# Layer norm: accumulated sums and ScalarE squares in place of VectorE's statistics

## Chip, cores and metric

The kernel runs on one core of a Trainium2 chip. The metric is the device time of one execution in microseconds, as the median of several runs. A profile of one execution goes with it; its span runs from the first recorded event to the last.

## What is computed

A two-layer decoder trunk on 512 tokens of width 1024, all in float32. Layer 1 is gated linear attention with memory cross-attention, layer 2 stick-breaking attention with memory cross-attention. After each mixer and after each PEER expert stage stands a layer norm over the scaled residual, four in all:

```python
def layer_norm(x, g, b):
    xf = x.astype(jnp.float32)
    mu = jnp.mean(xf, axis=-1, keepdims=True)
    var = jnp.mean(jnp.square(xf - mu), axis=-1, keepdims=True)
    return ((xf - mu) * lax.rsqrt(var + EPS) * g + b).astype(x.dtype)

for layer in range(DEPTH):
    mix = gla_layer_mixer(...) if layer < N_A_LAYERS else sb_layer_mixer(...)
    h = layer_norm(DEEPNORM_ALPHA * h + mix, ln_g[layer, 0], ln_b[layer, 0])
    ffn = peer(h, peer_w_q[layer], peer_subkeys[layer], peer_u[layer], peer_v[layer])
    h = layer_norm(DEEPNORM_ALPHA * h + ffn, ln_g[layer, 1], ln_b[layer, 1])
```

## The kernel before

The residual stream lies in SBUF as `E.x` (tile name `xnat`): 128 partitions, four token tiles of 128 tokens, 1024 columns each. For matmuls it is kept transposed as well, split into a high and a low float32r part (`xhi`, `xlo`), so that each product is three matmuls: high by high, low by high, high by low. `x_to_T` makes those parts of one token tile: eight transposes on TensorE (L813), the high part on ScalarE (L817), the low part on VectorE (L818).

`layer_norm(E, lp, t, halves, gam, bet)` works on one token tile, 128 rows of 1024. `halves` are the two 512-column halves of what is added to the residual, in PSUM (`oacc`, `acc`) or, for one tile, in SBUF (`va`). For each half VectorE forms `y = ALPHA*x + half` (L830) and takes its statistics (L831). One aggregate (L832) gives mean and variance, L834 adds epsilon, ScalarE takes the square root (L835), and VectorE meanwhile writes the centred and scaled `y` over itself (L836). The reciprocal (L837) is refined by one Newton step (L839 to L842), and L843 writes the result to `E.x`. The table for the root is asked for early by `warm_sqrt` (L847); where another table has been loaded in between, a load stands before the root.

It is called 16 times:

- `out_proj_ln`, after each mixer: the output projection runs tile by tile on TensorE (L248 to L252, into `oacc`), in an order written out by hand: tile t's matmuls, then the transposes of tile t-1, while tile t's norm runs on the other engines. After tile 3 TensorE first does the early part of the next stage's query projection (`pq`, L113 to L115, three tiles of tokens), and then tile 3's transposes. VectorE and ScalarE are ordered by the framework's scheduler there. The load of the next stage's keys (L998) stands on ScalarE's queue.
- `peer`, at the end of each stage, through `finish`. Token tile 0 is done by gathered expert rows, which VectorE accumulates into `va` (L985) after its dot products (L967); the other three tiles by dense matmuls over all 16384 experts (into `acc`). The last five expert blocks of every tile are held back, so that the tiles end one after the other: TensorE does tile 1's five blocks, its norm follows, then tile 2's, then tile 3's, with transposes of the finished tiles between. Tile 0's norm stands in the hand-written order of VectorE and ScalarE; those of the other tiles are ordered by the scheduler, which may weave them into it. In the second stage nothing is transposed, and each finished tile goes to the output by a transfer on SyncE's queue (L1320).

After the first PEER stage mixer B starts with weights that ScalarE and VectorE split as well (L93, L94) and whose first matmuls are `bsp`, L113 to L115.

Of the kernel before, what the change touches and what calls it, by code (L numbers as in the profile page):

```python
# [9 lines left out]
F32 = mybir.dt.float32  # L10
# [3 lines left out]
AF = mybir.ActivationFunctionType  # L14
ALU = mybir.AluOpType
AX = mybir.AxisListType
P = 128
T = 512
NT = 4
D = 1024  # L20
NC = 8
ALPHA = 4.0 ** 0.25
EPS = 1e-5
# [195 lines left out]
def out_proj_ln(E, cat, wo, lng, lnb, ahead, order=range(NC), rows=None):  # L219


    nc = E.nc
    with E.tc.tile_pool(name="lp", bufs=1, reuse_waits="tile") as lp:
        w = {}
        for c in order:
            w[c] = split(E, load_raw(E, wo[c], "wo"), "wo", lp, f"wo{c}", rows=None if rows is None or c >= GH else rows[:, c:c + 1])
        gam, bet = load_ln(E, lp, lng, lnb)
        warm_sqrt(E)
        next(ahead)
        with E.tc.manual_schedule(engines={mybir.EngineType.PE}):  # L230
            for t in range(NT + 1):
                if t < NT:
                    acc = [psum(E, name="oacc") for h in range(2)]
                    for c in order:
                        ch, cl = cat[c]
                        mov_mm(E, acc, ch[:, t * P:(t + 1) * P], cl[:, t * P:(t + 1) * P], *w[c], c == order[0], c == order[-1])
                if t == NT:
                    next(ahead)
                if t > 0:
                    x_to_T(E, t - 1)  # L240
                if t < NT:
                    layer_norm(E, lp, t, acc, gam, bet)
# [578 lines left out]
def layer_norm(E, lp, t, halves, gam, bet):  # L821

    nc = E.nc
    y = lp.tile([P, D], F32, tag="lny", name="lny", bufs=2)
    st = E.lnp.tile([P, 2, 6], F32, tag="lnst", name="lnst", bufs=2)
    mv = E.lnp.tile([P, 2], F32, tag="lnmv", name="lnmv", bufs=2)
    sm = E.lnp.tile([P, 4], F32, tag="lnsm", name="lnsm", bufs=2)
    for hf in range(2):
        sl = slice(hf * 512, (hf + 1) * 512)
        nc.vector.scalar_tensor_tensor(y[:, sl], E.x[:, t, sl], ALPHA, halves[hf], op0=ALU.mult, op1=ALU.add)  # L830
        nc.vector.bn_stats(st[:, hf], y[:, sl])  # L831
    nc.vector.bn_aggr(mv, st)  # L832
    ve, sd, r0, q = (sm[:, i:i + 1] for i in range(4))
    nc.vector.tensor_scalar(ve, mv[:, 1:2], EPS, None, op0=ALU.add)  # L834
    nc.scalar.activation(sd, ve, AF.Sqrt)  # L835
    nc.vector.scalar_tensor_tensor(y, y, mv[:, 0:1], gam, op0=ALU.subtract, op1=ALU.mult)  # L836
    nc.vector.reciprocal(r0, sd)  # L837

    nc.vector.tensor_mul(q, r0, r0)  # L839
    nc.vector.tensor_mul(q, q, ve)  # L840
    nc.vector.tensor_scalar(q, q, -0.5, 1.5, op0=ALU.mult, op1=ALU.add)
    nc.vector.tensor_mul(r0, r0, q)  # L842
    nc.vector.scalar_tensor_tensor(E.x[:, t], y, r0, bet, op0=ALU.mult, op1=ALU.add)  # L843
# [44 lines left out]
def peer(E, mixer, wq, sk, ut, vt, un, lng, lnb, out_dram=None):  # L888
# [6 lines left out]
    with ExitStack() as pp:  # L895
# [421 lines left out]
        def finish(t, halves):  # L1317
            layer_norm(E, wv, t, halves, *vp["ln"])
            if out_dram is not None:
                nc.sync.dma_start(out_dram[t * P:(t + 1) * P], E.x[:, t])  # L1320
# [154 lines left out]
```

## Time and profile before

| | |
|---|---|
| median of 3 runs | 3024.09 us (3017.12 to 3024.11) |
| the profiled execution | 3013.86 us |
| its span | 3012.1 us |
| TensorE matmul busy | 2930.4 us, 97% |
| VectorE busy | 2397.6 us, 80% |
| ScalarE busy | 1429.3 us, 47% |
| GpSimd busy | 646.5 us, 21% |

In the lines of the profile PE is TensorE's matmul, PEld its weight load, DVE VectorE, ACT ScalarE, POOL GpSimd, SP SyncE; a "q" behind the name is that engine's queue of waits and transfers. A timeline row gives the start in us, the duration in us, the engine, the line of the kernel, the operation, and "out<-in" by tile names with shapes; a bracket tells how long the engine had been idle before and which instruction released it. A row of a tile's list gives the count and the shortest, median and longest duration in ns. A busy TensorE is not TensorE at its peak; idle time of an engine that is not the bottleneck costs nothing. Instructions of one engine overlap slightly, so the distance from start to start is less than the duration.

### The profile page before, as it was taken

Reading aid. Unit: us, or ns where it says so; the run is one execution under the profiler, and the core shown is the slowest. Engines: PE = TensorE matmul, PEld = TensorE weight load, DVE = VectorE, ACT = ScalarE, POOL = GpSimd, SP = SyncE. Lnnn points to the kernel's source line nnn. Section 1 sums busy time; section 2 is a strip of 40 time slices with the busy share of each in tenths; the row PEclk is TensorE's granted clock in tenths of the full one; section 3 lists DMA queues with packets and bytes.
Section 4 is the critical chain, followed back from the end, with each engine's and each line's share of the span. In section 5 each row is a group of like instructions: output and inputs, shape, how many; then the busy total and the mean of one; then the engine's idle time right before and its main releaser. Section 6 shows DMA issues by size and latency. Waiting matters only on the chain.

```text
span 3012.1 us, 44494 instructions
## 1 busy us (share of the span) xinstructions
PE 2930.4 (97%) x16250; PEld 2589.2 (86%) x16250; DVE 2397.6 (80%) x5289; ACT 1429.3 (47%) x2482; POOL 646.5 (21%) x560
## 2 busy tenths in 40 slices
PE   9999999999999999999899899999999999999997
PEld 7878899999998888888676588999999998888886
DVE  5565899999876888787756658999999778787888
ACT  5342457676773333433235423466676643333332
POOL 0100131222323222322002000321213233223221
PEclk9999999999999999999899999999999999999999
DMA  4331488888999999999310223789889899999995
GB/s 175 112 105 63 155 294 316 320 313 318 334 336 323 308 346 357 347 352 346 126 63 29 76 79 119 276 309 323 304 324 321 330 330 333 338 341 347 369 341 190
DMA packets 314555, 789.91 MB, mean 262 GB/s; under 512 B 41808, under 2 KB 133984, under 8 KB 307936
## 3 DMA queue, kind: packets, MB, share of 16 engines
q1 hardware_dynamic: 216384, 419.48, 40.4%
q0 software_dynamic: 73728, 268.47, 25.2%
q10 hardware_dynamic: 24224, 99.13, 8.4%
q8 instruction: 127, 2.08, 0.3%
q14 instruction: 92, 0.75, 0.1%
HBM read 692.09 MB, written 94.90 MB: 261 GB/s over the span
## 4 chain that ended last, share of the span: by engine, by line
PE 91%; DVE 6%; issue 1%; DMA 1%; ACT 1%; ACTq 0%; SPq 0%; DVEq 0%
PE ph L113 11%; PE acc L248 11%; PE acc L250 11%; PE acc L252 11%; PE ph L115 11%; PE ph L114 11%; PE pq L114 2%; PE pq L115 2%; PE pq L113 2%; PE pg L1204 1%; PE pg L1205 1%; PE pss L1252 1%; PE bsp L113 1%; PE bsp L114 1%; PE bsp L115 1%
## 5 line engine op out<-in xcount | busy, mean ns | idle before, releaser
L113 PE MATMUL ph<-xhi,uh 128*128 128x384 f32 x2048 | 701.0, 342 | 0.0
L115 PE MATMUL ph<-xhi,ul 128*128 128x384 f32 x2048 | 686.3, 335 | 0.2
L114 PE MATMUL ph<-xlo,uh 128*128 128x384 f32 x2048 | 685.5, 335 | 0.0
L93 ACT ACTIVATE vh<-vr 128x1024 fp32r<-128x1024 f32 x256 | 271.5, 1060 | 597.0 <-issue 422.2
L932 POOL DMA_INDIRECT gr<-in_un,gidx x256 | 300.5, 1174 | 1023.2 <-DVE gr L967 806.8
L248 PE MATMUL acc<-vh,whi 128*128 128x512 f32 x1536 | 475.4, 391 | 8.9 <-ACT whi L1354 8.9
L250 PE MATMUL acc<-vl,whi 128*128 128x512 f32 x1536 | 474.4, 390 | 0.0
L252 PE MATMUL acc<-vh,wlo 128*128 128x512 f32 x1536 | 473.9, 390 | 0.0
L932 POOL DMA_INDIRECT gr<-in_vt,gidx x256 | 294.5, 1150 | 808.3 <-DVE va L985 736.8
L94 DVE TENSOR_TENSOR vl<-vr,vh 128x1024 fp32r<-128x1024 f32 x256 | 313.6, 1225 | 184.7 <-ACT vh L93 184.7
L93 ACT ACTIVATE uh<-ur 128x1024 fp32r<-128x1024 f32 x288 | 304.6, 1057 | 243.6 <-PE ph L114 234.1
L94 DVE TENSOR_TENSOR ul<-ur,uh 128x1024 fp32r<-128x1024 f32 x288 | 350.6, 1218 | 65.1 <-ACT uh L93 65.0
L114 PEld LDWEIGHTS ph<-xlo,uh 128*128 128x128 f32 x2048 | 386.0, 188 | 0.0
L113 PEld LDWEIGHTS ph<-xhi,uh 128*128 128x128 f32 x2048 | 385.7, 188 | 0.0
L115 PEld LDWEIGHTS ph<-xhi,ul 128*128 128x128 f32 x2048 | 385.0, 188 | 0.9 <-DVE ul L94 0.9
L248 PEld LDWEIGHTS acc<-vh,whi 128*128 128x128 f32 x1536 | 288.8, 188 | 70.6 <-ACT whi L1354 11.2
L250 PEld LDWEIGHTS acc<-vl,whi 128*128 128x128 f32 x1536 | 288.7, 188 | 61.2 <-DVE vl L94 1.3
L252 PEld LDWEIGHTS acc<-vh,wlo 128*128 128x128 f32 x1536 | 288.6, 188 | 60.5 <-DVE wlo L1355 0.9
L985 DVE SCALAR_TENSOR_TENSOR va<-gr,gw,va 128x1024 f32<-128x1024 f32 x254 | 325.3, 1281 | 15.7 <-DMA gr<-in_vt,gidx 15.4
L967 DVE SCALAR_TENSOR_TENSOR gr<-gr,xnat 128x1024 f32<-128x1024 f32 x256 | 310.4, 1214 | 11.7 <-DMA gr<-in_un,gidx 11.6
L1177 ACT ACTIVATE obl<-obh,rat 128x128 f16<-128x128 f16 x768 | 244.3, 393 | 20.0 <-ACT gt L1208 6.5
L1354 ACT ACTIVATE whi<-w 128x384 fp32r<-128x384 f32 x256 | 130.6, 510 | 59.5 <-DVE w L1351 59.5
(333 smaller groups left out, 4154.5 us busy)
## 6 DMA issues: line engine op xcount, KB each, us to landing
ur<-in_ut SPq DMA_DIRECT2D x256, 512.0 KB
vr<-in_vt SPq DMA_DIRECT2D x256, 512.0 KB
Gd<-gt ACTq DMA_DIRECT2D x48, 1024.0 KB
gl<-Gd SPq DMA_DIRECT2D x30, 1536.0 KB
Ad<-act ACTq DMA_DIRECT2D x108, 384.0 KB
al<-Ad SPq DMA_DIRECT2D x108, 384.0 KB
ur<-in_wq SPq DMA_DIRECT2D x32, 512.0 KB
bs<-in_b_st SPq DMA_DIRECT2D x14, 512.0 KB
```

Source lines behind the costliest of these rows:

```text
L93: nc.scalar.activation(hi, raw, AF.Copy)
L94: sub = lambda: eng.tensor_sub(lo, raw, hi.bitcast(F32))
L113: nc.tensor.matmul(ps, h, xhi[:, c, sl], start=(c == 0), stop=False)
L114: nc.tensor.matmul(ps, h, xlo[:, c, sl], start=False, stop=False)
L115: nc.tensor.matmul(ps, l, xhi[:, c, sl], start=False, stop=(c == NC - 1))
L248: nc.tensor.matmul(acc[hf], lh, hi[:, hf * 512:(hf + 1) * 512], start=first, stop=False)
L250: nc.tensor.matmul(acc[hf], lh, lo[:, hf * 512:(hf + 1) * 512], start=False, stop=False)
L252: nc.tensor.matmul(acc[hf], ll, hi[:, hf * 512:(hf + 1) * 512], start=False, stop=last)
L932: nc.gpsimd.indirect_dma_start(out=gr, out_offset=None, in_=tab, in_offset=bass.IndirectOffsetOnAxis(ap=gidx[:, k:k + 1], axis=0))
L967: nc.vector.scalar_tensor_tensor(gr, gr, 1.0, E.x[:, 0], op0=ALU.mult, op1=ALU.mult, accum_out=gh[:, k:k + 1])
L985: nc.vector.scalar_tensor_tensor(va, gr, gw[:, k:k + 1], va, op0=ALU.mult, op1=ALU.add)
L1177: nc.scalar.activation(obl[:, q], obh[:, q], AF.Copy, scale=rat[:, n0 + q:n0 + q + 1])
```

## The change

Only `layer_norm` changes. The two additions write out their row sums through their accumulator. One small step makes the negative mean from the two sums. ScalarE then squares `y` about the mean over all 1024 columns, with its own accumulator giving the sum of squares; the squares themselves go to `E.x[:, t]` as scratch, which the last step overwrites. VectorE centres and scales `y`, makes the variance with epsilon, ScalarE takes the root, and the Newton step has one instruction fewer, as one instruction forms the product of three. The statistics, the aggregate and two small tiles are gone.

```diff
     y = lp.tile([P, D], F32, tag="lny", name="lny", bufs=2)
-    st = E.lnp.tile([P, 2, 6], F32, tag="lnst", name="lnst", bufs=2)
-    mv = E.lnp.tile([P, 2], F32, tag="lnmv", name="lnmv", bufs=2)
-    sm = E.lnp.tile([P, 4], F32, tag="lnsm", name="lnsm", bufs=2)
+    sm = E.lnp.tile([P, 8], F32, tag="lnsm", name="lnsm", bufs=2)
+    s0, s1, nm, vs, ve, sd, r0, q = (sm[:, i:i + 1] for i in range(8))
     for hf in range(2):
         sl = slice(hf * 512, (hf + 1) * 512)
-        nc.vector.scalar_tensor_tensor(y[:, sl], E.x[:, t, sl], ALPHA, halves[hf], op0=ALU.mult, op1=ALU.add)
-        nc.vector.bn_stats(st[:, hf], y[:, sl])
-    nc.vector.bn_aggr(mv, st)
-    ve, sd, r0, q = (sm[:, i:i + 1] for i in range(4))
-    nc.vector.tensor_scalar(ve, mv[:, 1:2], EPS, None, op0=ALU.add)
+        nc.vector.scalar_tensor_tensor(y[:, sl], E.x[:, t, sl], ALPHA, halves[hf], op0=ALU.mult, op1=ALU.add, accum_out=sm[:, hf:hf + 1])
+    nc.vector.tensor_scalar(nm, s0, s1, -1.0 / D, op0=ALU.add, op1=ALU.mult)
+
+    nc.scalar.activation(E.x[:, t], y, AF.Square, bias=nm, accum_out=vs)
+    nc.vector.scalar_tensor_tensor(y, y, nm, gam, op0=ALU.add, op1=ALU.mult)
+    nc.vector.tensor_scalar(ve, vs, 1.0 / D, EPS, op0=ALU.mult, op1=ALU.add)
     nc.scalar.activation(sd, ve, AF.Sqrt)
-    nc.vector.scalar_tensor_tensor(y, y, mv[:, 0:1], gam, op0=ALU.subtract, op1=ALU.mult)
     nc.vector.reciprocal(r0, sd)
 
-    nc.vector.tensor_mul(q, r0, r0)
-    nc.vector.tensor_mul(q, q, ve)
+    nc.vector.scalar_tensor_tensor(q, r0, ve, r0, op0=ALU.mult, op1=ALU.mult)
     nc.vector.tensor_scalar(q, q, -0.5, 1.5, op0=ALU.mult, op1=ALU.add)
     nc.vector.tensor_mul(r0, r0, q)
     nc.vector.scalar_tensor_tensor(E.x[:, t], y, r0, bet, op0=ALU.mult, op1=ALU.add)
```

## The prediction

> **What bounds the kernel now.** I read the page's first and fourth parts, then the rows of the tiles that layer norm writes, then the timeline at each place where a layer norm runs.
>
> ```profile
> span 3012.1 us, 44494 instructions
> PE 2930.4 (97%) x16250; PEld 2589.2 (86%) x16250; DVE 2397.6 (80%) x5289; ACT 1429.3 (47%) x2482; POOL 646.5 (21%) x560
> PE 91%; DVE 6%; issue 1%; DMA 1%; ACT 1%; ACTq 0%; SPq 0%; DVEq 0%
> L831 DVE BATCH_NORM_STATS2 lnst<-lny x32: 674/683/694, 210.7 to 3002.4; 128x6 f32<-128x512 f32 x32
> L832 DVE BATCH_NORM_AGGREGATE lnmv<-lnst x16: 189/208/210, 212.1 to 3003.1; 128x2 f32<-128x12 f32 x16
> L836 DVE SCALAR_TENSOR_TENSOR lny<-lny,lnmv,gam x16: 1272/1276/1278, 212.4 to 3003.4; 128x1024 f32<-128x1024 f32 x16
> L839 DVE TENSOR_TENSOR lnsm<-lnsm x16: 146/159/161, 213.8 to 3006.0; 128x1 f32<-128x1 f32 x16
> ```
>
> TensorE carries 91% of the chain of waits; VectorE owns 6%. Only 16 layer norms run (four after each mixer, four at the end of each PEER stage), so the change can pay only where one of them holds up TensorE or the end. After a mixer it does not:
>
> ```profile
> 242.06 1.29 DVE L830 SCALAR_TENSOR_TENSOR lny<-xnat,oacc 128x512 f32<-128x512 f32 x2 [4.33 <-PE oacc L252]
> 243.35 1.29 DVE L818 TENSOR_TENSOR xlo<-xtp,xhi 128x512 fp32r<-128x512 f32 x2
> 244.10 0.44 PE L114 MATMUL pq<-xlo,uh 128*128 128x384 f32 x1 [0.29 <-DVE xlo L818]
> 244.56 1.28 DVE L831 BATCH_NORM_STATS2 lnst<-lny 128x6 f32<-128x512 f32 x2
> 246.11 0.15 DVE L834 TENSOR_SCALAR lnsm<-lnmv 128x1 f32<-128x1 f32 x1
> 246.18 1.28 DVE L836 SCALAR_TENSOR_TENSOR lny<-lny,lnmv,gam 128x1024 f32<-128x1024 f32 x1
> 246.36 0.20 ACT L835 ACTIVATE lnsm<-lnsm 128x1 f32<-128x1 f32 x1 [2.55 <-DVE lnsm L834]
> 247.37 0.16 DVE L837 RECIPROCAL lnsm<-lnsm 128x1 f32<-128x1 f32 x1
> 248.34 1.29 DVE L843 SCALAR_TENSOR_TENSOR xnat<-lny,lnsm,bet 128x1024 f32<-128x1024 f32 x1
> 256.52 1.03 PE L813 MATMUL xtp<-ident,xnat 128*128 128x128 f32 x8
> ```
>
> That is the last tile after mixer A. Its norm ends at 248.34 + 1.29 = 249.63, and TensorE asks for it at 256.52, 6.9 us later. From the sums at 242.06 to 249.63 are 7.57 us, of which 1.21 belong to the transposed tile's L818 (243.35 to 244.56): one norm alone takes **6.36 us**. The five small steps from L837 (247.37) to L843 (248.34) take 0.97 us, 0.19 each. At the end of the first PEER stage it is otherwise:
>
> ```profile
> 1460.58 0.69 DVE L830 SCALAR_TENSOR_TENSOR lny<-xnat,va 128x512 f32<-128x512 f32 x1
> 1461.19 0.68 DVE L830 SCALAR_TENSOR_TENSOR lny<-xnat,acc 128x512 f32<-128x512 f32 x1
> 1468.87 1.28 DVE L843 SCALAR_TENSOR_TENSOR xnat<-lny,lnsm,bet 128x1024 f32<-128x1024 f32 x1
> 1470.21 1.97 PE L813 MATMUL xtp<-ident,xnat 128*128 128x128 f32 x8 [5.89 <-DVE xnat L843]
> 1480.39 0.69 DVE L830 SCALAR_TENSOR_TENSOR lny<-xnat,acc 128x512 f32<-128x512 f32 x1
> 1481.66 1.28 DVE L843 SCALAR_TENSOR_TENSOR xnat<-lny,lnsm,bet 128x1024 f32<-128x1024 f32 x1
> 1488.46 1.28 DVE L843 SCALAR_TENSOR_TENSOR xnat<-lny,lnsm,bet 128x1024 f32<-128x1024 f32 x1
> 1489.89 1.94 PE L813 MATMUL xtp<-ident,xnat 128*128 128x128 f32 x8 [5.80 <-DVE idb L652]
> ```
>
> TensorE idles 5.89 us for tile 0 and 5.80 us for tile 3 (the row names a cast, but the tile came at 1488.46 + 1.28 = 1489.74, 0.15 before the transposes). Tile 0 takes 1460.58 to 1470.15, 9.57 us, because tile 1's norm is woven into it; tile 3 takes 1480.39 to 1489.74, 9.35 us. The kernel's end is the same without transposes:
>
> ```profile
> 2985.82 0.69 DVE L830 SCALAR_TENSOR_TENSOR lny<-xnat,va 128x512 f32<-128x512 f32 x1
> 2995.76 0.61 PE L252 MATMUL acc<-vh,wlo 128*128 128x512 f32 x2
> 2999.16 0.67 DVE L830 SCALAR_TENSOR_TENSOR lny<-xnat,acc 128x512 f32<-128x512 f32 x1
> 3006.79 1.28 DVE L843 SCALAR_TENSOR_TENSOR xnat<-lny,lnsm,bet 128x1024 f32<-128x1024 f32 x1
> ```
>
> TensorE is done at 2996.37, but tile 3's sums start only at 2999.16: VectorE has a queue. Four norms fill 2985.82 to 3008.07, 22.25 us or **5.56 us of VectorE per norm**, and the last output transfer ends the span 4.0 us later.
>
> **The change, part by part.** Prices that the norm itself does not show:
>
> ```profile
> L967 DVE SCALAR_TENSOR_TENSOR gr<-gr,xnat x256: 1194/1215/1236, 335.4 to 2434.6; 128x1024 f32<-128x1024 f32 x128
> L967 DVE DVE_READ_ACCUMULATOR gr<-gr,xnat x256: 72/81/96, 336.5 to 2435.8; 128x1 f32 x128
> L985 DVE SCALAR_TENSOR_TENSOR va<-gr,gw,va 128x1024 f32<-128x1024 f32 x254 | 325.3, 1281 | 15.7 <-DMA gr<-in_vt,gidx 15.4
> 203.74 1.15 ACT L96 ACTIVATE woh<-wo,hgc 128x1024 fp32r<-128x1024 f32 x1 [2.09 <-DMA wo<-in_a_wo]
> 1688.32 0.47 ACT L323 ACTIVATE mp<-msc,mnm 128x256 f32<-128x256 f32 x1 [2.09 <-DVE mnm L319]
> 1688.69 0.19 ACT L323 ACTIVATION_READ_ACCUMULATOR mp<-msc,mnm 128x1 f32 x1
> L514 ACT ACTIVATE sq<-po x6: 592/606/623, 153.3 to 174.1; 128x512 f32<-128x512 f32 x6
> L835 ACT ACT_TABLE_LOAD x2: 1283/1283/1283, 208.6 to 1737.9; - x2
> L589 ACT ACT_TABLE_LOAD x1 | 1.3, 1283 | 0.0
> 246.38 0.34 ACTq L998 DMA_DIRECT2D skt<-in_sk  x1
> 266.67 0.96 PE pss L1252 x8
> ```
>
> *VectorE, removed:* two statistics of 683 ns, which issue every 0.61 us like the sums (1460.58, 1461.19), 1.22 us; the aggregate (208 ns) and one product (159 ns), an estimated 0.12 us of issue each, as instructions overlap. About 1.45 us a norm.
>
> *VectorE, added:* two accumulator reads and the step that makes the negative mean. With accumulator L967 takes 1215 ns, without it L985 takes 1281 on the same shape, so the sum itself is free; the two reads cost between nothing and 2 x 0.08. The mean costs 0.07 to 0.12. Net about **1.25 us less** per norm (bounds 1.15 to 1.35): 5.56 becomes 4.3.
>
> [...]
>
> *ScalarE, added:* one pass over 1024 columns with a per-row operand. L96 is such a pass, 1.15 us; L323's read begins 0.37 us into a 0.47 us pass, so 0.1 before its end, and takes 0.19. Together **1.25 us**; a hand-over between engines costs at most 0.10 (the variance ends at 246.11 + 0.15, the root starts at 246.36). ScalarE was idle 2.55 us before the square root at 246.36, so the pass delays nothing of its own.
>
> *Moved, and the new wait:* the centred product (L836) overwrites y, which the squares read, so it must now wait for them, and the variance comes after. A norm alone becomes: sums 1.36 (1.29 and a read), mean 0.2, squares 1.25 with 0.1 for both hand-overs, product 1.19, variance, root and hand-overs 0.45, then reciprocal to final step 0.78 (0.97 less one step of 0.19) and the final 1.28: **6.6 us against 6.36**. If the variance is issued ahead of the product, the 0.45 hides under it and the norm takes 6.2. So the latency stays within 0.2; the gain is VectorE time, and shows only where two norms or other work share VectorE. Queued behind the waiting product are the norm's small steps, in the PEER stages also the transposed tile's L818 and the next weights' low parts.
>
> *After the mixers* (eight norms): 6.9 us of cover for tile 3, and TensorE's own matmuls for the others; without that cover each would cost its 0.2. But at 243.35 L818 follows the sums, and TensorE waited 0.29 for it at 244.10: reads and mean ahead of it delay it by 0 to 0.35. I take 0.15 twice, **+0.3**. The first norm's root needs a table load of 1.283 us, which can no longer run before the squares; it is covered as the norm is. The next stage's key load on ScalarE's queue (L998, 246.38), issued behind tile 3's root, goes up to 1.4 us later; its first matmul is at 266.67: nothing.
>
> *First PEER end, tile 0* (9.57 us): four sums woven, 4 x 0.61 and reads, 2.7; mean, squares, hand-overs 1.45; product 1.19; the other tile's product and the small steps 1.9; final 1.28: 8.5, or 7.8 if tile 0's sums go first. Bounds: 0 (all latency) to 2.5 (two norms' VectorE time). I take **-1.3**, nearer the woven order that the rows at 1460.58 and 1461.19 show.
>
> *Same end, tile 3* (9.35 us against 6.36 alone, so 3.0 of other work: tile 2's final 1.2, four L818 of 0.6). One or two L818 now fit into the wait for the squares, and tile 2's norm is shorter. Bounds 0 to 2.5; I take **-1.2**. TensorE follows both at once: what it waits for next is its own matmuls and the split weights, which are made before.
>
> *The end:* VectorE-bound, 4 x 4.3 = 17.2 instead of 22.25, -5.0; but TensorE ends at 2996.37, and one norm of 6.6 from there is 3003.0, also -5.0. Where both bind, some is lost: first tile's squares stall VectorE for about 0.7, and the dependent small steps of the last tile have nothing between them, 0.4. I take **-3.8**, bounds -1.5 (only one norm's saving survives) to -5.0. The output transfers move along.
>
> **Sum:** 0.3 - 1.3 - 1.2 - 3.8 = **-6.0 us**, bounds -0.8 (0.7, 0, 0, -1.5) to -10.0. The profiled execution took 3013.86 us; it would take 3007.9. The median of the three runs lies 10.2 above it, and by the same difference comes to 3024.09 - 6.0 = **3018.1**.
>
> **Rivals.** A: *all VectorE time is gained*, -10.0, 3014.1. For it: 5.56 us a norm is pure issue time. Against: ScalarE's pass has no cover at the start.
> B: *latency binds*, each exposed norm keeps its length, up to -2 remains, 3022 to 3024. For it: 6.6 against 6.36. Against: VectorE's backlog at 2999.16.
> C, slower: *VectorE's fixed order puts the product right behind the mean*, as L836 follows L834 by 0.07 at 246.18. It then sits through 1.35 us of squares in each of the eight norms at the PEER ends, 10.8 against 10.0 saved, and L818 stands behind it after both mixers, 0.2 + 1.35 + 1.19 each, 5.5: +6.3, 3030.4. It decides once the stall per norm passes the 1.25 saved. Against: the order weaves two tiles wherever both are open.
> D: *table reloads*: if squares and roots need different tables, two loads of 1.283 stand between tiles, at four pairs up to 10.3 us: 3028.4. L514's squares ran after the load for the gate's Silu (L589) without one of their own; none ran here on the root's. [...]
>
> **How the numbers follow.** Forecast 0.58 (own range 3014 to 3021); A 0.13, B 0.18, C 0.07, D 0.04. The three runs spread 7 us, 0.23%; so 0.3%, 9 us, is about what can be told from no change. Faster beyond it: most of A and the forecast's upper part with a lucky run, 0.22; slower: half of C and D with some spread, 0.06; the rest 0.72. Range: from A's 3014 less most of the spread, 3008, to B's end and part of C and D, 3026.
>
> **What would show it.** L818's wait after mixer A stays near 0.3; the 5.89 us idle becomes about 4.6 and the 5.80 some 4.6; the last L843 ends near 18.4 us after tile 0's first sum instead of 22.25; the squares take 1.15 with a read of 0.2; no new table load appears. VectorE's busy time falls by 16 x 1.4 us. Wrong if the product's wait for the squares is long and nothing is in front of it.

## The result, and the profile after

| | changed | before, same chip |
|---|---|---|
| median | 3055.19 us (3042.62 to 3057.96, 6 runs) | 3022.33 us (3015.23 to 3024.39, 6 runs) |
| ratio | 1.0105, 95% interval 1.0083 to 1.0126 | |
| profiled execution | 3056.22 us, span 3054.5 | 3013.86 us, span 3012.1 |

The kernel became some 33 us slower, where 6 us less were forecast. By its interval the ratio stands for 25 to 38 us.

The page of the changed kernel, first its span and busy times, then the rows of the dense expert stage (the matmuls `mov_mm` issues into `acc`: count, busy us, mean ns of one, idle before):

```profile
span 3054.5 us, 44511 instructions
...
PE 2977.9 (97%) x16250; PEld 2605.8 (85%) x16250; DVE 2382.0 (78%) x5273; ACT 1446.1 (47%) x2514; POOL 620.1 (20%) x560
...
PE 91%; DVE 6%; issue 1%; ACT 1%; DMA 1%; ACTq 0%; SPq 0%; DVEq 0%
...
L248 PE MATMUL acc<-vh,whi 128*128 128x512 f32 x1536 | 486.0, 398 | 10.2 <-ACT whi L1352 10.2
...
L250 PE MATMUL acc<-vl,whi 128*128 128x512 f32 x1536 | 485.3, 397 | 0.0
```

The first of these rows on the page before:

```profile
L248 PE MATMUL acc<-vh,whi 128*128 128x512 f32 x1536 | 475.4, 391 | 8.9 <-ACT whi L1354 8.9
```

VectorE lost 15.6 us of work, as the change means it to. But TensorE is busy 47.5 us longer with the same 16250 matmuls. The chain of waits has the same shares, so no new wait stands out. Some 33 of the 47.5 sit in three lines that the change does not touch (486.0 less 475.4, 485.3 less 474.4, 485.0 less 473.9). A fixed stretch of 300 us inside that stage of the first layer shows it best. Before, and then after (the columns are the stretch, its length, busy us and count of PE, PEld, DVE, ACT, POOL, then granted clock, DMA share and GB/s):

```profile
1100.00:1400.00 300.00, 300.00 (x1325) 248.50 (x1324) 241.63 (x291) 110.75 (x150) 79.87 (x69) 1.00 0.99 350
```

```profile
1100.00:1400.00 300.00, 300.00 (x1287) 241.73 (x1286) 233.42 (x282) 107.53 (x147) 68.18 (x67) 1.00 0.97 339
```

TensorE never idles in either, the granted clock is 1.00 in both, a weight load takes the same (248.50 / 1324 and 241.73 / 1286, both 0.188 us), and yet 38 matmuls fewer get through. From start to start, the records step by 226.67 ns before (227, 227, 226 in turn) and by 233.33 ns on average after. Over the 4608 matmuls of both layers' stages (three lines of 1536) that is 4608 x 6.67 ns = **30.7 us**: nearly the whole loss. VectorE and the DMAs do less in the same stretch, too (339 GB/s in place of 350); since TensorE never waits for them there, they follow it.

The layer norm itself did about what was forecast. The rows of its tile `lny` after (count, then shortest, median and longest ns):

```profile
L832 ACT ACTIVATE xnat<-lny,lnsm x16: 1135/1152/1154, 211.2 to 3044.6; 128x1024 f32<-128x1024 f32 x16
L832 ACT ACTIVATION_READ_ACCUMULATOR xnat<-lny,lnsm x16: 182/186/199, 212.2 to 3045.7; 128x1 f32 x16
...
L829 DVE SCALAR_TENSOR_TENSOR lny<-xnat,va x4: 685/688/691, 1485.1 to 3031.6; 128x512 f32<-128x512 f32 x4
L829 DVE DVE_READ_ACCUMULATOR lny<-xnat,va x4: 80/80/82, 1485.7 to 3032.2; 128x1 f32 x4
...
  ACT xnat L832: 11.8, 11
```

The last row says that VectorE's product waited for the squares 11 times, 11.8 us in all; eight of these, 1.31 to 1.37 each, are the norms after the mixers, where TensorE has work of its own. The mean, from the rows of the norm's small tile:

```profile
L830 DVE TENSOR_SCALAR lnsm<-lnsm x16: 204/206/214, 210.9 to 3044.3; 128x1 f32<-128x1 f32 x16
```

What TensorE waited for at the end of the first PEER stage, from the timeline after:

```profile
1493.09 1.63 PE L813 MATMUL xtp<-ident,xnat 128*128 128x128 f32 x8 [4.14 <-DVE lnsm L839]
...
1504.50 1.09 PE L813 MATMUL xtp<-ident,xnat 128*128 128x128 f32 x8 [0.88 <-DVE xnat L841]
...
1511.37 1.94 PE L813 MATMUL xtp<-ident,xnat 128*128 128x128 f32 x8 [5.77 <-DVE idb L652]
```

Tile 0's wait went from 5.89 to 4.14 us, tile 3's from 5.80 to 5.77.

Between the two programs TensorE's, SyncE's and GpSimd's instructions and their order are the same. What differs beside the norm is where tiles lie. The pool `lnp` shrank from 256 bytes per partition (`lnst` 2 x 64, `lnmv` 2 x 32, `lnsm` 2 x 32) to 64, so every tile allocated behind it starts 192 bytes lower. Among them are the stationary tiles of the slowed stage: in the compiled programs `whi` starts at 166336 before and 166144 after, `wlo` at 174016 and 173824. The moving tiles `vh` and `vl` (87744 and 100032) lie ahead of the pool and stayed.

### The profile page after: what moved, and what is told of

It reads as the page before. It is cut to its first block, busy times and chain, and to the rows that moved or that the text cites. A ratio compares the mean times of both kernels' runs of the same rounds, so it can differ in the third digit from the quotient of the medians.

```text
span 3054.5 us, 44511 instructions
## 1 busy us (share of the span) xinstructions
PE 2977.9 (97%) x16250; PEld 2605.8 (85%) x16250; DVE 2382.0 (78%) x5273; ACT 1446.1 (47%) x2514; POOL 620.1 (20%) x560
## 4 chain that ended last, share of the span: by engine, by line
PE 91%; DVE 6%; issue 1%; ACT 1%; DMA 1%; ACTq 0%; SPq 0%; DVEq 0%
PE acc L248 11%; PE ph L113 11%; PE acc L252 11%; PE acc L250 11%; PE ph L115 11%; PE ph L114 11%; PE pq L114 2%; PE pq L115 2%; PE pq L113 2%; PE pg L1202 1%; PE pg L1203 1%; PE pss L1250 1%; PE oacc L250 1%; PE oacc L252 1%; PE bsp L113 1%
## 5 line engine op out<-in xcount | busy, mean ns | idle before, releaser
L248 PE MATMUL acc<-vh,whi 128*128 128x512 f32 x1536 | 486.0, 398 | 10.2 <-ACT whi L1352 10.2
L250 PE MATMUL acc<-vl,whi 128*128 128x512 f32 x1536 | 485.3, 397 | 0.0
L252 PE MATMUL acc<-vh,wlo 128*128 128x512 f32 x1536 | 485.0, 397 | 0.0
L930 POOL DMA_INDIRECT gr<-in_vt,gidx x256 | 268.1, 1047 | 869.4 <-DVE va L983 794.3
L1206 ACT ACTIVATE gt<-pg 128x512 f32<-128x512 f32 x192 | 114.0, 594 | 80.7 <-PE pg L1203 44.3
```

The source lines that it names most:

```text
L248: nc.tensor.matmul(acc[hf], lh, hi[:, hf * 512:(hf + 1) * 512], start=first, stop=False)
L250: nc.tensor.matmul(acc[hf], lh, lo[:, hf * 512:(hf + 1) * 512], start=False, stop=False)
L252: nc.tensor.matmul(acc[hf], ll, hi[:, hf * 512:(hf + 1) * 512], start=False, stop=last)
L930: nc.gpsimd.indirect_dma_start(out=gr, out_offset=None, in_=tab, in_offset=bass.IndirectOffsetOnAxis(ap=gidx[:, k:k + 1], axis=0))
```

## The experiments

Every kernel below is read by the same row: the matmuls that get through between 1100 and 1400 us. Where a kernel was executed only once, that row decides and not the time: on one chip the 23 executions of the kernel before lie between 3012 and 3030 us.

**The changed kernel with the old addresses.** An unused tile fills the pool up to its old 256 bytes:

```diff
     E.lnp = ctx.enter_context(tc.tile_pool(name="lnp", bufs=1))
+    E.lnpad = E.lnp.tile([P, 48], F32, name="lnpad")
```

> The changed kernel with one unused tile of 192 B per partition in the pool of the norm's small tiles, so that every tile behind that pool lies at its old address; no instruction changes. Theory P (placement): the changed kernel's dense expert matmuls against acc step 233.3 ns instead of 226.7 because their SBUF tiles moved down by 192 B; with the pad they step 226.7 again, 4608 x 6.6 ns = 30 us come back, and the time is 3013 to 3022, at or a few us below before. Rival I (the instructions of the new norm, or the traffic that they cause): the step stays at 233.3 and the time at 3045 to 3057.

```profile
1100.00:1400.00 300.00, 300.00 (x1325) 248.51 (x1324) 242.24 (x291) 111.18 (x151) 71.78 (x69) 1.00 1.00 352
```

1325 matmuls again, and a median of 3015.27 us against 3019.05: ratio 0.9989 (0.9976 to 1.0003). The loss is gone with the address, and the new norm is all in: TensorE is busy for 2931.3 us, beside 2930.4 before and 2977.9 in the changed kernel. A longer timing of the same kernel:

> The changed kernel with 192 bytes per partition left free in the small layer-norm pool, so that every other tile has its address of before; a second, longer timing of it. Its profile so far shows three gains: 1.63 us at the first token tile of the first expert stage (idle 5.89 to 4.26), 0.66 at that stage's tile 2 (1.54 to 0.88), 2.76 at the kernel's end (first sum to end of last step 22.25 to 19.49). Theory A, these gains are all there is and all count: 5.05 us less than before, ratio 0.9983. Theory B, something else takes them back: ratio 1.000.

3012.70 against 3019.34 us, ratio 0.9976 (0.9961 to 0.9992): theory A's 0.9983 lies in both intervals. 1.000 lies outside this one, though just inside the shorter timing's.

**The kernel before, moved.** Nothing of the norm is changed; two of its small tiles are taken from another pool, so that everything else shifts as in the changed kernel:

```diff
-    st = E.lnp.tile([P, 2, 6], F32, tag="lnst", name="lnst", bufs=2)
-    mv = E.lnp.tile([P, 2], F32, tag="lnmv", name="lnmv", bufs=2)
+    st = lp.tile([P, 2, 6], F32, tag="lnst", name="lnst", bufs=2)
+    mv = lp.tile([P, 2], F32, tag="lnmv", name="lnmv", bufs=2)
```

> The kernel before, with the two statistics tiles taken out of the norm's small pool and put behind the other tiles of the stage, so that everything else lies 192 B lower, as in the changed kernel; its instructions are those of before. Theory P: the acc matmuls step 233.3 ns and the time is 3045 to 3062. Rival I: 226.7 ns and 3015 to 3025.

```profile
1100.00:1400.00 300.00, 300.00 (x1287) 240.43 (x1286) 233.15 (x282) 107.92 (x147) 68.36 (x67) 1.00 0.97 339
```

3052.03 against 3019.05 us, ratio 1.0120 (1.0087 to 1.0154), with the old arithmetic. So the move alone makes the loss; the squares, the accumulators and the new waits have no part in it.

**Only the weights moved back.** 192 bytes are left free right ahead of `whi`; all the rest stays moved:

```diff
             w = wv.tile([P, TD], F32, tag="w", name="w")
+            if i == 0:
+                wv.tile([P, 48], F32, tag="wpad", name="wpad", bufs=1)
             whi = wv.tile([P, TD], F32R, tag="whi", name="whi", bufs=TAIL)
```

> The changed kernel with 192 B unused between the tiles w and whi in the dense expert stage: the stationary tiles whi and wlo (and the activations, gains and norm tiles behind them) are at their old addresses, while the gathered rows, keep, w and everything of the other stages stay 192 B lower. If the address of the stationary tiles sets the step: 226.7 ns and about 3018 to 3025. If it is another moved tile (the gather buffers, the activations kept in SBUF, w): 233.3 ns and about 3050.

```profile
1100.00:1400.00 300.00, 300.00 (x1325) 248.39 (x1325) 239.36 (x289) 110.46 (x150) 69.33 (x68) 1.00 0.99 349
```

Fast, 3017.84 us: of all that moved, the stationary tiles (and what lies behind them in their pool) decide.

**A third address.** The first edit with 16 in place of 48 columns; everything then lies 128 bytes lower than before in place of 192.

> The changed kernel with an unused tile of 64 B in the small pool, so that everything behind it lies 128 B lower than before instead of 192 B. Theory P says only that the step depends on the address; if a boundary of 128 B decides (before whi lay 64 B behind one, in the changed kernel on one, here again 64 B behind one), 226.7 ns; if it is one of 256 B or 512 B, anything between 226.7 and 233.3. Rival I: 233.3 ns, about 3050.

```profile
1100.00:1400.00 300.00, 300.00 (x1287) 241.35 (x1286) 233.14 (x281) 107.86 (x147) 68.25 (x67) 1.00 0.98 338
```

Slow, 3037.47 us with 1287: a start on a 64-byte or 128-byte boundary is not what counts.

**Four further placements, to find the rule.** The first two vary the free bytes ahead of `whi` (32 and 64 columns in the weights' edit):

> The changed kernel with 128 bytes per partition left free between the w tile and the stationary tiles whi and wlo of the dense expert stage; nothing else moves. It places whi at 384 modulo 512 bytes, where the kernel before has it at 448, the changed kernel at 256, and the kernel shifted by 128 bytes less had it at 320. Step of the dense stage's matmuls so far: 226.67 ns at 448; 233.33 ns at 256 and 320. Theory 1, the stationary tile's address relative to the moving tile's must be at least 256 bytes apart in a 512-byte window (before: 256 apart, fast; 64 and 128 apart, slow): here they are 192 apart, so the step stays 233.33 ns and the time near 3046 us. Theory 2, only the 128-byte quarter from 384 to 511 of the stationary address is fast: 226.67 ns, time near 3017 us, 30.7 us less (4608 matmuls x 6.67 ns).

```profile
1100.00:1400.00 300.00, 300.00 (x1312) 246.17 (x1311) 238.56 (x287) 108.83 (x148) 68.92 (x68) 1.00 0.98 345
```

> The changed kernel with 256 bytes per partition left free between the w tile and the stationary tiles whi and wlo; whi comes to 0 modulo 512 bytes, 320 away from the moving tiles vh and vl (192 modulo 512). Theory 1 (a distance of 256 or more to the moving tile is fast): 226.67 ns a step, time near 3017 us. Theory 2 (only a stationary address in the quarter from 384 to 511 is fast): 233.33 ns, near 3046 us.

```profile
1100.00:1400.00 300.00, 300.00 (x1287) 240.45 (x1286) 233.25 (x282) 107.81 (x147) 68.47 (x67) 1.00 0.97 339
```

The first fits neither theory: 1312 matmuls, a step of 228.89 ns, a third of the loss (3027.16 us, beside 3021.94 of the kernel before). The second, slow at 3043.25 us, fells theory 1 as worded (a distance of 256 or more is free). The next one moves the moving tiles:

```diff
+    E.hlpad = ctx.enter_context(tc.tile_pool(name="hlpad", bufs=1)).tile([P, 48], F32, name="hlpad")
     E.hl = ctx.enter_context(tc.tile_pool(name="hl", bufs=3))
```

> The changed kernel with 192 bytes per partition left free ahead of the moving operands' pool (tiles vh, vl and all behind them). The stationary tiles whi and wlo come back to the addresses of the kernel before (448 modulo 512), but the moving tiles go 192 bytes further up as well (384 modulo 512 instead of 192), so that their distance is 64 again as in the changed kernel. Theory 1 (the distance between stationary and moving tile decides): the step stays 233.33 ns, time near 3048 us. Theory 2 (the stationary tile's own address decides): 226.67 ns, near 3017 us.

```profile
1100.00:1400.00 300.00, 300.00 (x1287) 241.70 (x1287) 233.73 (x281) 107.19 (x147) 67.83 (x67) 1.00 0.98 339
```

Slow, 3053.80 us, although the weights are at the very address that was fast before: the moving tiles' place counts as well, as theory 1 has it. And `wlo` alone, by moving the free bytes behind `whi`:

> The changed kernel with 192 bytes per partition left free between whi and wlo, so that wlo alone (and what lies behind it) has the address of the kernel before; whi stays at the changed kernel's. If each matmul's step hangs on the addresses of its own two tiles: a third of the 4608 matmuls (those of line 252, vh by wlo) return to 226.67 ns and two thirds stay at 233.33, time some 10 us below the changed kernel, near 3040. If instead another tile behind wlo, or the whole pool's place, decides: all three lines go the same way, 226.67 ns and near 3017 us, or 233.33 ns and near 3048 us.

```profile
1100.00:1400.00 300.00, 300.00 (x1294) 242.41 (x1293) 234.91 (x284) 107.42 (x147) 68.22 (x67) 1.00 0.98 340
```

1294 and 3042.66 us, a mean step of 232.22 ns: a sixth of the loss is gone where a third was expected, so a matmul's step is not set by its own two tiles alone. Why a sixth stays open.

**Both tiles moved, and a distance of 0.** The moving tiles' 192 bytes and the weights' 192 together; then 448 bytes ahead of the weights alone:

> The changed kernel with 192 bytes per partition left free ahead of the moving operands' pool and 192 more between the w tile and the stationary tiles. Both addresses are new (moving 384, stationary 128 modulo 512 bytes), but their distance is 256 bytes in a 512-byte window, as in the kernel before. So far the step is 226.67 ns at a distance of 256, 228.89 at 192, and 233.33 at 64, 128 and 320. Theory 1 (the distance between stationary and moving tile decides, 256 is free): 226.67 ns, time near 3017 us. Theory 2 (the absolute addresses decide, each in its own way): no reason for just this pair to be fast; 233.33 ns, near 3048 us, as with the pair 384 and 448.

> The changed kernel with 448 bytes per partition left free between the w tile and the stationary tiles whi and wlo: stationary and moving tile then both lie at 192 modulo 512 bytes, a distance of 0. Measured so far, step by distance: 226.67 ns at 256 (two pairs of addresses), 228.89 at 192, 233.33 at 64, 128 and 320. Theory 1a (the loss grows the nearer the two tiles are in the 512-byte window): at least 233.33 ns, time 3045 us or more. Theory 1b (only distances that are no multiple of 256 lose): 226.67 ns, near 3017 us. For 1b speaks that the matmuls of the first expert half (tiles xhi and uh) show no loss.

The first of the two, then the second:

```profile
1100.00:1400.00 300.00, 300.00 (x1325) 248.57 (x1324) 240.84 (x290) 110.05 (x150) 72.46 (x69) 1.00 1.00 350
```

```profile
1100.00:1400.00 300.00, 300.00 (x1326) 248.48 (x1325) 241.06 (x290) 110.00 (x150) 71.09 (x69) 1.00 1.00 349
```

Both are fast (3021.74 and 3016.08 us, beside 3019.34 and 3015.12 of the kernel before). The absolute addresses of the first are all new, and still it is fast, which theory 2 gives no reason for. 1b is the form that is left: what counts is the stationary tile's place relative to the moving tile's. By stationary address less moving address, modulo 256 bytes:

| offset | kernels | step |
|---|---|---|
| 0 | before, padded change, weights only, both moved, distance 0 | 226.67 ns |
| 64 | changed, moved before, weights + 256, moving tiles moved | 233.33 ns |
| 128 | third address | 233.33 ns |
| 192 | weights + 128 | 228.89 ns |

The two kernels whose moving tiles were shifted show it at a second place, and a limit. The weights of the mixers' projections (`asp`, `bsp`) and of the first expert half (`ph`) lie in the shifted pool; what they are multiplied with, `xhi` and `xlo`, did not move. So these matmuls have an offset of 192 in those two kernels and of 0 in all others. Waits left out, the 512-column matmuls into `asp` and `bsp` step by 229 ns there in the median, and by 227 in each of the twelve others. The 384-column matmuls into `ph` show no loss that can be told: in the first layer they take 587.7 us from first to last in both kernels, 585.6 to 588.8 in the others, where 2.22 ns each would add 6.8.

**A better version.** The old addresses, with the squares written to a tile of their own and the product to the residual tile, so that the product need not wait for the squares:

```diff
-    nc.scalar.activation(E.x[:, t], y, AF.Square, bias=nm, accum_out=vs)
-    nc.vector.scalar_tensor_tensor(y, y, nm, gam, op0=ALU.add, op1=ALU.mult)
+    sq = lp.tile([P, D], mybir.dt.bfloat16, tag="lnsq", name="lnsq", bufs=1)
+    nc.scalar.activation(sq, y, AF.Square, bias=nm, accum_out=vs)
+    nc.vector.scalar_tensor_tensor(E.x[:, t], y, nm, gam, op0=ALU.add, op1=ALU.mult)
...
-    nc.vector.scalar_tensor_tensor(E.x[:, t], y, r0, bet, op0=ALU.mult, op1=ALU.add)
+    nc.vector.scalar_tensor_tensor(E.x[:, t], E.x[:, t], r0, bet, op0=ALU.mult, op1=ALU.add)
```

> The changed kernel with 192 bytes left free in the layer-norm pool (all other tiles at the addresses of before), and with the squares written to a bfloat16 scratch tile of their own; VectorE writes the centred product straight to the residual tile and no longer waits for the squares that read y. Measured in the profile of the kernel without this edit: one norm alone 6.61 us, of which the product of 1.20 us stands behind squares of 1.25 us. Theory A, the wait is on the path: a norm alone falls to some 5.4 us, tile 0's idle of 4.26 us and the kernel's end of 19.49 us by about 0.5 to 1.2 each, 1 to 3 us in all against that kernel. Theory B, VectorE's own time binds: only its stalls for the squares at the expert stages' ends go, 0.46 twice and 0.17, under 1.1 us and no difference that can be told.

Its timeline, TensorE at the end of the first PEER stage, then VectorE's first sum and last step of the kernel:

```profile
1473.03 1.09 PE L814 MATMUL xtp<-ident,xnat 128*128 128x128 f32 x8 [3.74 <-DVE lnsm L841]
...
1483.65 1.09 PE L814 MATMUL xtp<-ident,xnat 128*128 128x128 f32 x8 [0.20 <-DVE xnat L843]
...
1490.62 1.73 PE L814 MATMUL xtp<-ident,xnat 128*128 128x128 f32 x7 [5.88 <-DVE idb L653]
...
2984.51 0.69 DVE L830 SCALAR_TENSOR_TENSOR lny<-xnat,va 128x512 f32<-128x512 f32 x1
...
3001.34 1.28 DVE L843 SCALAR_TENSOR_TENSOR xnat<-xnat,lnsm,bet 128x1024 f32<-128x1024 f32 x1
```

The end takes 18.11 us in place of 19.49, tile 0's wait 3.74 in place of 4.26, tile 2's 0.20 in place of 0.88, tile 3's 5.88 in place of 5.76: 2.5 us less in the profile. One norm alone, at mixer A's last tile, takes 5.39 us (245.21 to 251.81, less 1.21 for the transposed tile's step). Both are as theory A has them. The time is 3010.37 us against 3019.34, ratio 0.9973 (0.9960 to 0.9987), which beats the kernel before; against the padded change's 0.9976 it can't be told apart.

## Why the prediction was wrong

It failed at one step: "The change, part by part" prices instructions and waits only, and has no term for the smaller tiles, which so count for nothing in the sum of -6.0. The diff says that two tiles are gone and one has changed size, and their pool stands ahead of the weights' in SBUF. That moved the stationary tiles of two stages whose 4608 matmuls take a third of the time (4608 x 226.67 ns is 1044 us), and cost 30.7 us, six times the gain of the norm. None of the rivals was this one: C and D, the slower ones, lie in the norm, where nothing was lost. The measured loss of 33 us is 30.7 less the norm's gain, plus a remainder of some 7 that the intervals (25 to 38 us here, 26 to 46 for the moved kernel before) are too wide to confirm.

With the same instructions, the step is 226.67 or 233.33 ns by where the one tile lies relative to the other. No run here shows why.

Apart from that step, the padded change is the test of the prediction, since in it only the norm differs from before. The forecast's ratio, 0.9980, lies in both of its intervals, but so does any gain from 2.4 to 7 us; the terms have to be read from the profile. Its timeline at mixer A's last tile, at the end of the first PEER stage, and at the kernel's end:

```profile
242.26 0.69 DVE L830 SCALAR_TENSOR_TENSOR lny<-xnat,oacc 128x512 f32<-128x512 f32 x1 [4.08 <-PE oacc L253]
...
243.56 1.29 DVE L819 TENSOR_TENSOR xlo<-xtp,xhi 128x512 fp32r<-128x512 f32 x2
...
244.31 0.44 PE L115 MATMUL pq<-xlo,uh 128*128 128x384 f32 x1 [0.29 <-DVE xlo L819]
...
244.76 0.20 DVE L831 TENSOR_SCALAR lnsm<-lnsm 128x1 f32<-128x1 f32 x1
...
248.79 1.28 DVE L842 SCALAR_TENSOR_TENSOR xnat<-lny,lnsm,bet 128x1024 f32<-128x1024 f32 x1
...
1463.93 1.28 DVE L834 SCALAR_TENSOR_TENSOR lny<-lny,lnsm,gam 128x1024 f32<-128x1024 f32 x1 [0.46 <-ACT xnat L833]
...
1468.56 1.97 PE L814 MATMUL xtp<-ident,xnat 128*128 128x128 f32 x8 [4.26 <-DVE lnsm L840]
...
1478.72 0.69 DVE L830 SCALAR_TENSOR_TENSOR lny<-xnat,acc 128x512 f32<-128x512 f32 x1
...
1480.67 1.09 PE L814 MATMUL xtp<-ident,xnat 128*128 128x128 f32 x8 [0.88 <-DVE xnat L842]
...
1486.10 1.28 DVE L842 SCALAR_TENSOR_TENSOR xnat<-lny,lnsm,bet 128x1024 f32<-128x1024 f32 x1
...
1487.53 1.94 PE L814 MATMUL xtp<-ident,xnat 128*128 128x128 f32 x8 [5.76 <-DVE idb L653]
...
2983.38 0.69 DVE L830 SCALAR_TENSOR_TENSOR lny<-xnat,va 128x512 f32<-128x512 f32 x1
...
3001.59 1.28 DVE L842 SCALAR_TENSOR_TENSOR xnat<-lny,lnsm,bet 128x1024 f32<-128x1024 f32 x1
```

And the transposes of tile 2 before:

```profile
1482.99 1.09 PE L813 MATMUL xtp<-ident,xnat 128*128 128x128 f32 x8 [1.54 <-DVE xnat L843]
```

| term | predicted | measured | from |
|---|---|---|---|
| after the mixers | +0.3 | 0 | the wait for the transposed tile is 0.29 as before; the norm still ends 6.7 us ahead of need |
| first PEER end, tile 0 | -1.3 | -1.63 | 5.89 to 4.26 |
| same end, later tiles | -1.2 | -0.70 | tile 3's 5.80 to 5.76; tile 2's 1.54 to 0.88 |
| kernel's end | -3.8 | -2.76 | 22.25 to 19.49 |
| sum | -6.0 | -5.1 | |

One norm alone takes 7.81 us from 242.26 to 250.07, less the transposed tile's step between (1.20): 6.61, as worked out (6.6). Tile 0's sums now go first, the case for which the prediction had 7.8 us; its norm takes 7.94 (1460.57 to 1468.51). Tile 3's norm takes 8.66 us (1478.72 to 1487.38) in place of 9.35, 0.69 less where 1.2 was forecast; TensorE's waits show that gain almost wholly at tile 2's transposes, which stand just before tile 3's. At the end the stretch of the four norms shows the mis-sized term, before and then padded:

```profile
2985.81:3008.08 22.27, 10.56 (x47) 8.43 (x45) 22.04 (x52) 0.81 (x4) 0.00 (x0) 0.85 0.17 68
```

```profile
2983.37:3002.88 19.51, 10.55 (x47) 8.41 (x45) 18.14 (x48) 5.65 (x12) 0.00 (x0) 0.83 0.20 81
```

VectorE's work fell by 22.04 - 18.14 = 3.90 us, 0.98 a norm and not 1.25, outside the bounds of 1.15 to 1.35. Its idle time rose by 1.1 (0.23 to 1.37), as much as the 0.7 and 0.4 that were set aside together. So the price of the norm's VectorE work was too hopeful, the loss at the ends right in sum. Counting each instruction of these two stretches up to the next one's start, or to its own end if that is earlier, two terms stand out: the mean takes 0.18 us a norm where 0.07 to 0.12 was taken, and the product of three 0.20 where the two it replaces took 0.23, so that 0.03 was saved there and not 0.12. Over the whole kernel VectorE's busy time fell by 17.5 us (2397.6 to 2380.1), not by 16 x 1.4 = 22.4.

The norm's sums bear out that the accumulator is nearly free: those with both sources in SBUF take 688 ns with it (the rows of L829 above), 682 without. The row of before:

```profile
L830 DVE SCALAR_TENSOR_TENSOR lny<-xnat,va x4: 673/682/692, 1460.6 to 2987.6; 128x512 f32<-128x512 f32 x4
```

Rival D fell: the root's table is loaded five times before and after (1283 ns each), and the squares, which ran ahead of such a load in the first norm and behind it in the next, brought none of their own. Rival C fell: at the PEER ends the product's longest wait for the squares was 0.46 us, and after mixer A the transposed tile's step (243.56) went ahead of the mean (244.76), not behind the product.

## What to carry to other kernels

A diff that changes the size of any tile in a long-lived pool moves every tile behind it; before the time of such a change is read, compare the addresses, or pad the pool to its old size, so that only the change is measured. Where TensorE is the bound, look at the matmuls that did not change: the same count, the clock at 1.00, no idle time, but fewer per microsecond, was a matter of placement here, and a pad shows whether it is. In these runs an offset of a multiple of 256 bytes between the stationary and the moving tile was free.

## What the runs showed of the hardware

- A 128x512 matmul with its weight load steps in 226.67 ns or in 233.33 ns by the placement of two tiles. With offsets of 64 and 128 bytes modulo 256 the step is 6.67 ns longer, with 192 it is 2.22 ns longer. A second group of 512-column matmuls lost about as much at 192 (median step 229 ns against 227), 384-column ones at 192 lost nothing that can be told. Offsets that are no multiple of 64 were not tried.
- With one of two weight tiles at a free offset and the other at 64 bytes, only a sixth of the loss went (232.22 ns), which the simple rule doesn't explain.
- In the changed kernel's profiled execution the granted clock fell to 0.56 and 0.58 between 260 and 280 us, where it was 1.00 in the kernel before. This cost some 8 us there (the first expert stage's first matmul starts at 362.36 us, not at 354.57), part of why its span is 42 us longer and the median only 33. Two of the other profiled executions have such a spell at the same place, four have one near 1800 us, and eight of the fourteen have none so long; the longer timing of the padded kernel has both, its first timing none. No run tells what sets them off. The two stretches after:

```profile
260.00:270.00 10.00, 10.00 (x55) 10.00 (x54) 1.23 (x1) 1.54 (x2) 0.00 (x0) 0.56 0.17 52
270.00:280.00 10.00, 8.82 (x36) 7.85 (x36) 2.46 (x3) 4.06 (x6) 0.00 (x0) 0.58 0.16 52
```

- ScalarE's squares with per-row operand and accumulator over 1024 columns took 1152 ns, the read of the accumulator 186; VectorE's read of its accumulator 80 to 85 ns, overlapped with the next sum (both start at 208.04 us in the first norm).
